# Feed-forward pairs by seven products: one bank for four of them, copies between on ScalarE, and other pairs

## The chip, the cores and the metric

The kernel runs on one core of a Trainium2 chip. The metric is device time in microseconds of one execution, on the device alone. The core's engines are TensorE (PE in the profile; its weight loads are PEld), VectorE (DVE), ScalarE (ACT), GpSimd (POOL) and SyncE (SP), which issues most transfers. Each engine works through its own queue in order, and semaphores hold an instruction until what it needs is there.

## The reference, cut to what matters

Two layers of a streaming encoder over 512 tokens of width 1024. Each has a mixer, a cross-attention to a memory and a gated feed-forward network with a short convolution along the tokens; the change touches the last one alone:

```python
def conv_ffn(xn, w_up, conv_w, conv_b, w_down):
    h = causal_depthwise_conv(xn @ w_up, conv_w) + conv_b
    g, u = jnp.split(h, 2, axis=-1)
    return (jax.nn.gelu(g) * u) @ w_down
...
        x = x + conv_ffn(rms_norm(x, ffn_norm[layer]), ffn_w_up[layer], ffn_conv_w[layer],
                         ffn_conv_b[layer], ffn_w_down[layer])
```

All is float32. w_up has 1024 rows and 2 x 2816 columns, so h has 44 blocks of 128 columns; block p of the gate half and block 22 + p of the other half are a pair, and there are 22 pairs. w_down takes the 22 blocks of the product back to 1024.

## The kernel before, in words

Everything is kept transposed: 128 features on the partitions, 512 tokens along the free axis. A float32 product is done as three matmuls (`mm3`, lines 285 to 291): each operand is split into a rounded high half (a cast on ScalarE) and the rest (a subtraction on VectorE, `sub`, line 279), and high x high, low x high and high x low are summed in a PSUM bank.

`ffn_steps` (line 1136) does a layer's feed-forward. It first lists tasks, each with an engine, an assumed duration, what it depends on, a priority (its due time) and buffer slots that it takes and frees; then `Sched.run` (line 181) simulates the engines and issues the instructions in the order that comes out. At each step it takes, over all engines, the task that can start first, by priority where several can. So the order of every engine's queue comes from the planner's durations, and TensorE's tasks of one pair can be put between those of another.

A pair is computed in one of two ways. `plain` (line 1308) runs two blocks of 8 x 3 matmuls of 512 tokens, each evacuated by one VectorE product with the norm's factor (line 1317). `seven` (line 1327) treats the pair as a 2 x 2 product (two column blocks by two halves of the 1024 rows, against two halves of the tokens) and does it with seven products of 4 x 3 matmuls of 256 tokens. It needs sums of weights: S2 and S4 (lines 1358 and 1364, VectorE) and f1, which GpSimd's queue adds up in a transfer (`onto`, line 1335, tile `sa`), and sums of the input, `th` and `tl`, which `forms` (line 1240) makes once per layer with two ScalarE scalings, three VectorE sums and a split per row block, four times.

In `seven` the products run in the order p1, p6, p2, a fill, p7, p5, a fill, p4, p3. Bank X takes p1 and p2, bank Y p6, p7 and p4, bank R p5 and p3. ScalarE copies p1 as v with its sign turned (line 1390) before p2 is added to it, and copies c11 out of X (line 1405). Every other partial result is a VectorE sum of a bank and a copy (`sum_`, line 1392): u2 and u3 go to buffers, c22, c21 and c12 to the rows of `hs`. p2 waits for v, p7 for u2, p4 for u3, p3 for c22, because each adds into a bank that must have been read before. Then one VectorE product scales all rows (line 1419), and `tail` does the convolution (ScalarE line 1274, four VectorE steps line 1281), the gelu (line 1289), the product (line 1291) and its split into `ah` and `al` (lines 1295 and 279).

A fill (line 1441) takes one block of the down projection from a queue: 4 x 3 matmuls of 512 with a 512-column cast, its low half and an add into x. The queue gets eight blocks at pairs 5, 9, 13 and 18; the last four are held back until after pair 21. Every pair from 5 on asks for two fills, so pairs 17, 20 and 21 find the queue empty. Pairs 4 to 15 and 17 to 20 go by `seven`, the others by `plain`. After the pairs come the four held blocks, then in layer one eight more blocks of six, and in layer two `finish` (line 1656), which needs the acts of pairs 16 to 21.

Of the kernel before, what the change touches and what calls it, by code (L numbers as in the profile page):

```python
# [13 lines left out]
ALU = mybir.AluOpType  # L14
# [8 lines left out]
NPAIR = DFF // P  # L23
CHUNKS = [(0, 4), (4, 4), (8, 4), (12, 4), (16, 6)]

SEVEN = (4, 5, 6, 7, 8, 9, 10, 11, 12, 13, 14, 15, 17, 18, 19, 20)
EPS = 1e-6

X_AT, X_STEP = 2.6, 0.6
# [37 lines left out]
def folded(ap):  # L67

    return ap.rearrange("p (r k) -> p r k", r=2)
# [168 lines left out]
class Builder:  # L238
# [897 lines left out]
    def ffn_steps(self, layer, mp):  # L1136
# [103 lines left out]
        def forms(k, at):  # L1240

            st = {}

            def scaled(j):
                if j == 0:
                    st["t"] = hs2[st["_hs"]][:, :, 2:514]
                nc.scalar.activation(st["t"][:, j, :512], self.x[k + 4 * j][:], AF.Identity, scale=self.col("ffn", layer * 8 + k + 4 * j))

            def first():
                st["r"] = raw_tile(st, "sa")[:]  # L1250
                tt_(out=pair(st["r"][:, :512]), in0=pair(st["t"][:, 0, :512]), in1=st["t"][:, :, 256:512], op=ALU.subtract)

            T1, T3, T2, T4 = (slice(256 * i, 256 * i + 256) for i in range(4))
            tt_ = nc.vector.tensor_tensor
            a = add("ACT", ACV, lambda: scaled(0), (), at, [("hs", st)])
            a = add("ACT", ACV, lambda: scaled(1), [a], at)
            a = add("DVE", tt(512), first, [a], at, [("sa", st)])
            a = add("DVE", tt(256), lambda: tt_(out=st["r"][:, T2], in0=st["t"][:, 1, 256:512], in1=st["r"][:, T1], op=ALU.add), [a], at)
            a = add("DVE", tt(256), lambda: tt_(out=st["r"][:, T4], in0=st["t"][:, 1, 0:256], in1=st["r"][:, T2], op=ALU.subtract), [a], at, (), [("hs", st)])
            h = add("ACT", act(1024), lambda: nc.scalar.copy(th[k][:], st["r"]), [a], at)  # L1260
            formed.append(add("DVE", tt(1024), lambda: self.sub(tl[k][:], st["r"], th[k][:]), [h], at, (), [("sa", st)]))

# [64 lines left out]
        def seven(p, fill):  # L1327
# [57 lines left out]
            n = 1.345  # L1385
            get = rows(st, at + 2.0)

            def v_():
                st["v_"] = self.til(mp, "v", (P, 256), bufs=1)
                nc.scalar.activation(folded(st["v_"][:]), bank("X")(), AF.Copy, scale=-1.0)  # L1390

            def sum_(tag, out, a, b, op):
                if tag:
                    st[tag] = self.til(mp, tag, (P, 256), bufs=1)
                tt_(out=out(), in0=a(), in1=b(), op=op)

            bank = lambda n_: (lambda: restored(st[n_][:, :256]))
            tmp = lambda n_: (lambda: folded(st[n_][:]))
            hs = lambda j, l: (lambda: folded(st["hs_"][:, j, 2 + 256 * l : 258 + 256 * l]))
            p1 = pe(n, lambda: opened("X", bx, "acc", f3, 0, *X(0, 0), "X", True), [w3], [("acc", bx)])  # L1400
            v = add("ACT", act(256), v_, [p1], clock[0], [("v", bv)])
            p6 = pe(n, lambda: opened("Y", by, "acc", s2, 0, *T2, "Y", True), [w2, *formed], [("acc", by)], [("s2", s2)])
            u2 = add("DVE", 0.33, lambda: sum_("u2", tmp("u2"), bank("Y"), tmp("v_"), ALU.add), [p6, v], clock[0], [("u2", bu2)])
            p2 = pe(n, lambda: product(f3, 512, *X(1, 0), "X", False), [p1, v], (), [("h", f3)])
            c11 = add("ACT", act(256), lambda: nc.scalar.copy(hs(0, 0)(), bank("X")()), [p2, get], clock[0] + 2.0, (), [("acc", bx)])
            fill()
            p7 = pe(n, lambda: product(f1, 0, *T3, "Y", False), [u2, w1])
            u3 = add("DVE", 0.33, lambda: sum_("u3", tmp("u3"), bank("Y"), tmp("v_"), ALU.add), [p7], clock[0], [("u3", bu3)])
            p5 = pe(n, lambda: opened("R", br, "s", f1, 512, *T1, "R", True), [w1], [("s", br)], [("h", f1)])
            c22 = add("DVE", 0.33, lambda: sum_(None, hs(1, 1), tmp("u3"), bank("R"), ALU.subtract), [u3, p5, get], clock[0], (), [("u3", bu3)])  # L1410
            fill()
            p4 = pe(n, lambda: product(a22, 0, *T4, "Y", False), [u3, w22], (), [("a22", a22)])
            c21 = add("DVE", 0.33, lambda: sum_(None, hs(1, 0), bank("Y"), tmp("v_"), ALU.add), [p4, get], clock[0] + 1.0, (), [("acc", by), ("v", bv)])
            p3 = pe(n, lambda: product(s4, 0, *X(1, 1), "R", False), [c22, w4], (), [("s4", s4)])
            c12 = add("DVE", 0.33, lambda: sum_(None, hs(0, 1), bank("R"), tmp("u2"), ALU.subtract), [p3, get], clock[0], (), [("s", br), ("u2", bu2)])

            def scaled():
                h = st["hs_"][:, :, 2:514]
# [29 lines left out]
        for p in range(22):  # L1448
            if p in due:
                queue += [(due[p], m) for m in range(8)]  # L1450
            if p == 19:
                queue, late = queue[:-4], queue[-4:]
            (seven if p in SEVEN else plain)(p, fill if p >= 5 else lambda: None)
            if p < 2:
                for k in (2 * p, 2 * p + 1):
                    forms(k, clock[0] + 4.0 * (k % 2))
# [376 lines left out]
```

## Time and profile before

| | |
|---|---|
| device time of the runs | 1451.02, 1455.0 and 1483.01 us, median 1455.0 |
| the profiled execution | 1451.45 us, its span 1449.6 us |
| granted TensorE clock, mean | 0.998 |
| TensorE, VectorE, ScalarE busy | 1423.5, 1189.9, 798.5 us |
| stretch 404.5 to 739.7 us (feed-forward of layer one) | 335.2 us: TensorE 329.73, VectorE 312.80, ScalarE 184.90 busy |
| stretch 1103.5 to 1406.7 us (pairs of layer two and the four held blocks) | 303.2 us: TensorE 298.80, VectorE 290.74, ScalarE 169.97 busy |

The profile is of one execution. Times within it count from the first instruction. A row of its timeline has the start, the duration, the engine, the line of the kernel, the operation, output and inputs by their names in the program with their shapes, and in brackets the idle time just before with what ended it. TensorE's matmuls are pipelined and their ends are modelled, so the next one can start before the end that is shown; the distance of two starts is the pace. VectorE's and ScalarE's instructions overlap their neighbours by a little too.

### The profile page before, as it was taken

How to read it: one execution, taken by the hardware profiler on the slowest of the kernel's cores; microseconds unless marked ns; L12 is line 12 of the kernel's file. 1: busy time of each engine (PE TensorE's matmuls, PEld its weight loads, DVE VectorE, ACT ScalarE, POOL GpSimd, SP SyncE). 2: the span in 40 equal slices, each digit the busy share in tenths (PEclk: the TensorE clock that was granted, in tenths of full speed). 3: DMA queues.
4: the chain of work that ended last, by engine and by line, in shares of the span. 5: the costliest groups of instructions: out<-in, count | busy, mean ns of one | idle time of the engine just before them, and what ended most of it. 6: DMA issues, size and time to landing. Idle time of an engine off the chain costs nothing.

```text
span 1449.6 us, 22210 instructions
## 1 busy us (share of the span) xinstructions
PE 1423.5 (98%) x8330; PEld 1266.7 (87%) x8330; DVE 1189.9 (82%) x2255; ACT 798.5 (55%) x1345; POOL 58.4 (4%) x100
## 2 busy tenths in 40 slices
PE   9999999999999999999999999999999999999998
PEld 7888868899888999989888788889988899998997
DVE  7778886766689999989778868677667999999985
ACT  7767574444466555545456734444445665554544
POOL 0000120000001000000000100000000000000000
PEclk9999999999999999999999999999999999999999
DMA  5222305323247565642332232324323765654322
GB/s 201 88 73 73 102 30 160 117 88 131 83 142 198 152 170 163 164 127 68 90 102 87 74 102 74 116 88 129 119 81 130 187 168 162 172 153 134 92 70 80
DMA packets 60795, 171.74 MB, mean 118 GB/s; under 512 B 6672, under 2 KB 6672, under 8 KB 60688
## 3 DMA queue, kind: packets, MB, share of 16 engines
q1 hardware_dynamic: 55072, 152.43, 32.5%
q0 software_dynamic: 4608, 16.78, 6.9%
q8 instruction: 65, 1.06, 0.3%
q10 hardware_dynamic: 1008, 1.12, 0.2%
q14 instruction: 42, 0.34, 0.1%
HBM read 168.21 MB, written 2.10 MB: 117 GB/s over the span
## 4 chain that ended last, share of the span: by engine, by line
PE 72%; DVE 19%; issue 4%; ACT 3%; DMA 2%; POOL 0%; SPq 0%; DVEq 0%; ACTq 0%; POOLq 0%
PE acc L289 14%; PE acc L291 14%; PE acc L290 14%; DVE wl L279 4%; PE w L289 4%; PE w L291 4%; PE w L290 4%; DVE c L1281 3%; PE acc L351 2%; PE acc L352 2%; PE acc L353 2%; PE s L289 2%; PE s L291 2%; PE s L290 2%; PE w L1620 1%
## 5 line engine op out<-in xcount | busy, mean ns | idle before, releaser
L289 PE MATMUL acc<-xh,wh 128*128 128x512 f32 (+1 forms) x832 | 293.6, 353 | 4.2 <-ACT v L1390 4.2
L291 PE MATMUL acc<-xh,wl 128*128 128x512 f32 (+1 forms) x832 | 289.0, 347 | 0.0
L290 PE MATMUL acc<-xl,wh 128*128 128x512 f32 (+1 forms) x832 | 289.0, 347 | 0.0
L279 DVE TENSOR_TENSOR wl<-raw,wh 128x1024 fp32r<-128x1024 f32 (+2 forms) x201 | 240.3, 1196 | 38.0 <-ACT wh L282 35.8
L282 ACT CAST wh<-raw 128x1024 fp32r<-128x1024 f32 (+2 forms) x137 | 140.3, 1026 | 155.8 <-PE acc L290 96.8
L289 PEld LDWEIGHTS acc<-xh,wh 128*128 128x128 f32 x832 | 158.2, 190 | 19.5 <-ACT v L1390 4.8
L291 PEld LDWEIGHTS acc<-xh,wl 128*128 128x128 f32 x832 | 158.1, 190 | 15.3
L290 PEld LDWEIGHTS acc<-xl,wh 128*128 128x128 f32 x832 | 158.3, 190 | 14.4
L1281 DVE SCALAR_TENSOR_TENSOR c<-hs,vec,c 128x512 f32<-128x512 f32 x176 | 128.8, 745 | 6.6 <-ACT c L1274 6.2
L289 PE MATMUL w<-ah,wh 128*128 128x512 f32 x304 | 115.4, 380 | 0.0
L290 PE MATMUL w<-al,wh 128*128 128x512 f32 x304 | 115.3, 379 | 0.0
L291 PE MATMUL w<-ah,wl 128*128 128x512 f32 x304 | 115.3, 379 | 0.0
L1274 ACT ACTIVATE c<-hs,vec 128x512 f32<-128x512 f32 x88 | 67.9, 808 | 64.2 <-DVE hs L1419 57.1
L291 PEld LDWEIGHTS w<-ah,wl 128*128 128x128 f32 x304 | 57.5, 189 | 8.1
L290 PEld LDWEIGHTS w<-al,wh 128*128 128x128 f32 x304 | 57.6, 190 | 6.7
L289 PEld LDWEIGHTS w<-ah,wh 128*128 128x128 f32 x304 | 57.7, 190 | 6.7
L1295 ACT CAST ah<-c 128x512 fp32r<-128x512 f32 x44 | 27.3, 620 | 65.7 <-DVE c L1291 65.6
L289 PE MATMUL acc<-mem,wh 128*128 128x256 f32 (+1 forms) x192 | 60.3, 314 | 0.0
L291 PE MATMUL acc<-mem,wl 128*128 128x256 f32 (+1 forms) x192 | 59.7, 311 | 0.0
L290 PE MATMUL acc<-mem,wh 128*128 128x256 f32 (+1 forms) x192 | 59.6, 311 | 0.0
L512 DVE TENSOR_TENSOR x<-w,x 128x512 f32<-128x512 f32 x72 | 49.1, 682 | 7.9 <-PE w L291 7.8
L512 DVE TENSOR_TENSOR x<-acc,x 128x512 f32<-128x512 f32 x32 | 22.0, 690 | 40.4 <-PE acc L291 40.4
(373 smaller groups left out, 3766.0 us busy)
## 6 DMA issues: line engine op xcount, KB each, us to landing
raw<-in_up_dram SPq DMA_DIRECT2D x56, 512.0 KB, 3.3
dr<-in_down_dram SPq DMA_DIRECT2D x64, 256.0 KB, 3.4
sa<-in_up_dram SPq DMA_DIRECT2D x32, 512.0 KB, 4.2
sa<-in_up_dram POOLq DMA_DIRECT2D x32, 512.0 KB, 5.5
raw<-in_xk_dram SPq DMA_DIRECT2D x16, 512.0 KB, 3.3
raw<-in_wo_dram SPq DMA_DIRECT2D x16, 512.0 KB, 3.3
raw<-in_xq_dram SPq DMA_DIRECT2D x16, 512.0 KB, 3.3
raw<-in_xv_dram SPq DMA_DIRECT2D x16, 512.0 KB, 3.3
```

Of the source, the lines that this page charges most:

```text
L279: self.nc.vector.tensor_tensor(out=lo, in0=v, in1=hi.bitcast(F32), op=ALU.subtract)
L282: self.nc.scalar.copy(hi, v)
L289: mm(out, wh, xh, start=first, stop=False, skip_group_check=parts)
L290: mm(out, wh, xl, start=False, stop=False, skip_group_check=parts)
L291: mm(out, wl, xh, start=False, stop=last, skip_group_check=parts)
L351: mm(ps, xh[k][:, ts], wh, start=(k == 0), stop=False)
L352: mm(ps, xh[k][:, ts], wl, start=False, stop=False)
L353: mm(ps, xl[k][:, ts], wh, start=False, stop=(k == 7))
L512: self.nc.vector.tensor_tensor(out=x, in0=restored(ps[:]), in1=x, op=ALU.add)
L1274: nc.scalar.activation(st["c_"][:, j, :], hs()[:, j, 2:514], AF.Identity, scale=self.col("cw", (layer * 3 + 2) * 44 + blk), bias=self.col( ...
L1281: nc.vector.scalar_tensor_tensor(out=c, in0=hs()[:, j, n : n + 512], scalar=w, in1=c, op0=ALU.mult, op1=ALU.add)
L1295: nc.scalar.copy(acts[p][0][:], u())
```

## The change

Bank Y now takes p1, p6, p7 and p4 one after the other. The signs in `forms` are chosen so that the bank itself holds each partial result; ScalarE copies it out between the products: v (p1), u2, u3 with the sign turned, and c21 with the sign turned straight into `hs`. Bank X holds p2 alone and VectorE adds v to it for c11; c22 and c12 stay VectorE sums. The order becomes p1, p2, p6, a fill, p5, p7, a fill, p4, p3; p6 waits for v, p7 for u2, p4 for u3, p3 for c22. In `forms` one VectorE difference of 512 columns becomes two of 256, and the two sums become operations with a factor of -1. The pairs by `seven` become 5 to 20 in layer one and 5 to 21 in layer two; so pair 4 is plain, pair 16 is by seven, and pair 21 too in layer two. The planner gets the new durations, dependencies and slots, and makes its order anew.

```diff
--- before.py
+++ after.py
@@ -23,7 +23,7 @@
 NPAIR = DFF // P
 CHUNKS = [(0, 4), (4, 4), (8, 4), (12, 4), (16, 6)]
 
-SEVEN = (4, 5, 6, 7, 8, 9, 10, 11, 12, 13, 14, 15, 17, 18, 19, 20)
+SEVEN = (range(5, 21), range(5, 22))
 EPS = 1e-6
 
 X_AT, X_STEP = 2.6, 0.6
@@ -1248,15 +1248,19 @@
 
             def first():
                 st["r"] = raw_tile(st, "sa")[:]
-                tt_(out=pair(st["r"][:, :512]), in0=pair(st["t"][:, 0, :512]), in1=st["t"][:, :, 256:512], op=ALU.subtract)
+                tt_(out=st["r"][:, T1], in0=st["t"][:, 0, 0:256], in1=st["t"][:, 0, 256:512], op=ALU.subtract)
+                tt_(out=st["r"][:, T3], in0=st["t"][:, 1, 256:512], in1=st["t"][:, 0, 256:512], op=ALU.subtract)
+
+            def second(to, a, b):
+                nc.vector.scalar_tensor_tensor(out=st["r"][:, to], in0=st["r"][:, a], scalar=-1.0, in1=st["t"][:, 1, b], op0=ALU.mult, op1=ALU.subtract)
 
             T1, T3, T2, T4 = (slice(256 * i, 256 * i + 256) for i in range(4))
             tt_ = nc.vector.tensor_tensor
             a = add("ACT", ACV, lambda: scaled(0), (), at, [("hs", st)])
             a = add("ACT", ACV, lambda: scaled(1), [a], at)
-            a = add("DVE", tt(512), first, [a], at, [("sa", st)])
-            a = add("DVE", tt(256), lambda: tt_(out=st["r"][:, T2], in0=st["t"][:, 1, 256:512], in1=st["r"][:, T1], op=ALU.add), [a], at)
-            a = add("DVE", tt(256), lambda: tt_(out=st["r"][:, T4], in0=st["t"][:, 1, 0:256], in1=st["r"][:, T2], op=ALU.subtract), [a], at, (), [("hs", st)])
+            a = add("DVE", 2 * tt(256), first, [a], at, [("sa", st)])
+            a = add("DVE", 0.4, lambda: second(T2, T1, slice(256, 512)), [a], at)
+            a = add("DVE", 0.4, lambda: second(T4, T2, slice(0, 256)), [a], at, (), [("hs", st)])
             h = add("ACT", act(1024), lambda: nc.scalar.copy(th[k][:], st["r"]), [a], at)
             formed.append(add("DVE", tt(1024), lambda: self.sub(tl[k][:], st["r"], th[k][:]), [h], at, (), [("sa", st)]))
 
@@ -1385,34 +1389,33 @@
             n = 1.345
             get = rows(st, at + 2.0)
 
-            def v_():
-                st["v_"] = self.til(mp, "v", (P, 256), bufs=1)
-                nc.scalar.activation(folded(st["v_"][:]), bank("X")(), AF.Copy, scale=-1.0)
-
-            def sum_(tag, out, a, b, op):
-                if tag:
-                    st[tag] = self.til(mp, tag, (P, 256), bufs=1)
+            def copied(tag, scale):
+                st[tag] = self.til(mp, tag, (P, 256), bufs=1)
+                nc.scalar.activation(folded(st[tag][:]), bank("Y")(), AF.Copy, scale=scale)
+
+            def sum_(out, a, b, op):
                 tt_(out=out(), in0=a(), in1=b(), op=op)
 
             bank = lambda n_: (lambda: restored(st[n_][:, :256]))
             tmp = lambda n_: (lambda: folded(st[n_][:]))
             hs = lambda j, l: (lambda: folded(st["hs_"][:, j, 2 + 256 * l : 258 + 256 * l]))
-            p1 = pe(n, lambda: opened("X", bx, "acc", f3, 0, *X(0, 0), "X", True), [w3], [("acc", bx)])
-            v = add("ACT", act(256), v_, [p1], clock[0], [("v", bv)])
-            p6 = pe(n, lambda: opened("Y", by, "acc", s2, 0, *T2, "Y", True), [w2, *formed], [("acc", by)], [("s2", s2)])
-            u2 = add("DVE", 0.33, lambda: sum_("u2", tmp("u2"), bank("Y"), tmp("v_"), ALU.add), [p6, v], clock[0], [("u2", bu2)])
-            p2 = pe(n, lambda: product(f3, 512, *X(1, 0), "X", False), [p1, v], (), [("h", f3)])
-            c11 = add("ACT", act(256), lambda: nc.scalar.copy(hs(0, 0)(), bank("X")()), [p2, get], clock[0] + 2.0, (), [("acc", bx)])
+            AC = 0.42
+            p1 = pe(n, lambda: opened("Y", by, "acc", f3, 0, *X(0, 0), "Y", True), [w3], [("acc", by)])
+            v = add("ACT", AC, lambda: copied("v", 1.0), [p1], clock[0], [("v", bv)])
+            p2 = pe(n, lambda: opened("X", bx, "acc", f3, 512, *X(1, 0), "X", True), [w3], [("acc", bx)], [("h", f3)])
+            c11 = add("DVE", 0.33, lambda: sum_(hs(0, 0), bank("X"), tmp("v"), ALU.add), [p2, v, get], clock[0] + 2.0, (), [("acc", bx), ("v", bv)])
+            p6 = pe(n, lambda: product(s2, 0, *T2, "Y", False), [w2, v, *formed], (), [("s2", s2)])
+            u2 = add("ACT", AC, lambda: copied("u2", 1.0), [p6], clock[0], [("u2", bu2)])
             fill()
-            p7 = pe(n, lambda: product(f1, 0, *T3, "Y", False), [u2, w1])
-            u3 = add("DVE", 0.33, lambda: sum_("u3", tmp("u3"), bank("Y"), tmp("v_"), ALU.add), [p7], clock[0], [("u3", bu3)])
-            p5 = pe(n, lambda: opened("R", br, "s", f1, 512, *T1, "R", True), [w1], [("s", br)], [("h", f1)])
-            c22 = add("DVE", 0.33, lambda: sum_(None, hs(1, 1), tmp("u3"), bank("R"), ALU.subtract), [u3, p5, get], clock[0], (), [("u3", bu3)])
+            p5 = pe(n, lambda: opened("R", br, "s", f1, 512, *T1, "R", True), [w1], [("s", br)])
+            p7 = pe(n, lambda: product(f1, 0, *T3, "Y", False), [u2, w1], (), [("h", f1)])
+            u3 = add("ACT", AC, lambda: copied("u3", -1.0), [p7], clock[0], [("u3", bu3)])
+            c22 = add("DVE", 0.33, lambda: sum_(hs(1, 1), tmp("u3"), bank("R"), ALU.subtract), [u3, p5, get], clock[0], (), [("u3", bu3)])
             fill()
             p4 = pe(n, lambda: product(a22, 0, *T4, "Y", False), [u3, w22], (), [("a22", a22)])
-            c21 = add("DVE", 0.33, lambda: sum_(None, hs(1, 0), bank("Y"), tmp("v_"), ALU.add), [p4, get], clock[0] + 1.0, (), [("acc", by), ("v", bv)])
+            c21 = add("ACT", AC, lambda: nc.scalar.activation(hs(1, 0)(), bank("Y")(), AF.Copy, scale=-1.0), [p4, get], clock[0] + 1.0, (), [("acc", by)])
             p3 = pe(n, lambda: product(s4, 0, *X(1, 1), "R", False), [c22, w4], (), [("s4", s4)])
-            c12 = add("DVE", 0.33, lambda: sum_(None, hs(0, 1), bank("R"), tmp("u2"), ALU.subtract), [p3, get], clock[0], (), [("s", br), ("u2", bu2)])
+            c12 = add("DVE", 0.33, lambda: sum_(hs(0, 1), bank("R"), tmp("u2"), ALU.add), [p3, get], clock[0], (), [("s", br), ("u2", bu2)])
 
             def scaled():
                 h = st["hs_"][:, :, 2:514]
@@ -1450,7 +1453,7 @@
                 queue += [(due[p], m) for m in range(8)]
             if p == 19:
                 queue, late = queue[:-4], queue[-4:]
-            (seven if p in SEVEN else plain)(p, fill if p >= 5 else lambda: None)
+            (seven if p in SEVEN[layer] else plain)(p, fill if p >= 5 else lambda: None)
             if p < 2:
                 for k in (2 * p, 2 * p + 1):
                     forms(k, clock[0] + 4.0 * (k % 2))
```

## The prediction

> **What bounds the kernel now.** I read the page first (span, busy shares, slices), then the stretches of the two feed-forward stages, then TensorE's rows one by one with what released each late one.
>
> ```profile
> span 1449.6 us, 22210 instructions
> ...
> PE 1423.5 (98%) x8330; PEld 1266.7 (87%) x8330; DVE 1189.9 (82%) x2255; ACT 798.5 (55%) x1345; POOL 58.4 (4%) x100
> ...
> DVE  7778886766689999989778868677667999999985
> ACT  7767574444466555545456734444445665554544
> ```
>
> TensorE is busy for 98% of the span. VectorE stands at 9 in the slices of the two feed-forward stages (404 to 740 us and 1103 to 1407 us) and at 6 to 8 elsewhere. A window over one period of a middle pair, one pair's seven products with two blocks of the down projection, and one over each disturbed end, show how close the two engines run there. The columns are busy time and count by engine, then clock, DMA share and GB/s.
>
> ```profile
> core 0: us, PE busy (x) PEld busy (x) DVE busy (x) ACT busy (x) POOL busy (x), PEclk, DMA share, GB/s
> 447.00:462.00 15.00, 12.16 (x101) 11.59 (x100) 13.76 (x22) 7.69 (x14) 1.70 (x2) 1.00 0.80 197
> 547.59:562.17 14.58, 14.58 (x111) 13.85 (x109) 14.51 (x24) 8.11 (x14) 0.84 (x1) 1.00 0.62 160
> 1337.00:1351.00 14.00, 11.78 (x103) 11.39 (x102) 12.32 (x20) 6.94 (x13) 0.87 (x1) 1.00 0.56 150
> ```
>
> In the middle TensorE is never idle (14.58 of 14.58 us) and VectorE hardly is (14.51); ScalarE has 6.5 us free. At the two ends TensorE loses time. TensorE's pace is read from the starts of its products:
>
> ```profile
> 567.53 0.38 PE L289 MATMUL w<-ah,wh 128*128 128x512 f32 x1
> ...
> 570.12 0.27 PE L289 MATMUL acc<-th,wh 128*128 128x256 f32 x1
> ...
> 571.46 0.28 PE L289 MATMUL s<-th,wh 128*128 128x256 f32 x1
> ```
>
> Twelve matmuls of 512 columns take 570.12 - 567.53 = 2.59 us, twelve of 256 columns 571.46 - 570.12 = 1.34 us. A seven-product pair (84 of 256) is then 7 x 1.34 = 9.38 us, a plain pair (48 of 512) 4 x 2.59 = 10.36 us. All late products of the pairs, with the idle time and its releaser in brackets:
>
> ```profile
> 449.89 0.28 PE L291 MATMUL s<-th,wl 128*128 128x256 f32 x1
> 452.86 0.38 PE L289 MATMUL acc<-xh,wh 128*128 128x256 f32 x1 [2.69 <-ACT v L1390]
> ...
> 531.56 0.38 PE L289 MATMUL acc<-th,a22h 128*128 128x256 f32 x1 [0.40 <-DVE u L1395]
> ...
> 620.90 0.38 PE L289 MATMUL s<-xh,s4h 128*128 128x256 f32 x1 [0.29 <-DVE hs L1395]
> ...
> 643.82 0.38 PE L289 MATMUL acc<-th,wh 128*128 128x256 f32 x1 [1.71 <-DVE u L1395]
> ...
> 1150.22 0.38 PE L289 MATMUL acc<-xh,wh 128*128 128x256 f32 x1 [1.05 <-ACT v L1390]
> ...
> 1228.94 0.38 PE L289 MATMUL acc<-th,a22h 128*128 128x256 f32 x1 [0.42 <-DVE u L1395]
> ...
> 1318.32 0.38 PE L289 MATMUL s<-xh,s4h 128*128 128x256 f32 x1 [0.33 <-DVE hs L1395]
> ...
> 1338.65 0.38 PE L289 MATMUL acc<-xh,wh 128*128 128x256 f32 x1 [0.51 <-ACT v L1390]
> ...
> 1341.98 0.38 PE L289 MATMUL acc<-th,wh 128*128 128x256 f32 x1 [1.72 <-DVE u L1395]
> ```
>
> The brackets sum to 9.12 us. A bracket counts from a row's modelled end (0.28 us) though the next matmul could start after 0.11, so each of the nine hides 0.17 us more: 10.7 us in all. The first layer's 452.86 and the second's 1150.22 belong to the start of the seven-product pairs (pair 4, which has no fill); 531.56 and 1228.94 are single late u3; 620.90, 643.82, 1318.32, 1338.65 and 1341.98 lie around plain pair 16 and pair 17, which has no fill either. So the stage is at TensorE's pace, with 10.7 us of stalls that VectorE, or ScalarE behind it, causes.
>
> **The change part by part.** *TensorE's work.* Pair 4 becomes plain and pair 16 seven in both layers: they cancel. Pair 21 of layer two becomes seven: 9.38 - 10.36 = **-0.98 us**. Its loads grow from 1024 to 1792 KB on SP's and POOL's queues, and pair 16's likewise; the middle window above carries just that load (0.62 of the DMA engines) with no stall of TensorE, so I price the transfers at nothing. If that cover were gone, up to a whole load's landing would show, the last column here (us):
>
> ```profile
> raw<-in_up_dram SPq DMA_DIRECT2D x56, 512.0 KB, 3.3
> ...
> sa<-in_up_dram POOLq DMA_DIRECT2D x32, 512.0 KB, 5.5
> ```
>
> *Sums moved between engines.* Per pair VectorE loses u2, u3 and c21 and gets c11, five sums to three; ScalarE goes from two copies to four.
>
> ```profile
> L1395 DVE TENSOR_TENSOR u<-acc,v x64: 409/417/424, 457.3 to 1385.3; 128x256 f32<-128x256 f32 x64
> ```
>
> ```profile
> L1390 ACT ACTIVATE v<-acc x32: 360/383/392, 452.4 to 1378.1; 128x256 f32<-128x256 f32 x32
> ...
>   PE acc L291: 15.8, 19
>   DVE hs L1395: 6.4, 6
> ```
>
> ```profile
> 1376.87 0.41 DVE L1395 TENSOR_TENSOR hs<-acc,v 128x256 f32<-128x256 f32 x1
> 1377.20 0.68 DVE L279 TENSOR_TENSOR a22l<-ra,a22h 128x512 fp32r<-128x512 f32 x1
> 1377.80 0.41 DVE L1395 TENSOR_TENSOR hs<-s,u 128x256 f32<-128x256 f32 x1
> ```
>
> A queued sum takes its engine for 0.33 us (1377.20 - 1376.87), a 512 one for 0.60; two sums less are 0.66 us a pair. VectorE's load with fills falls from 14.51 to 13.85 us against TensorE's 14.58; ScalarE's rises from 8.11 by at most 2 x 0.38 to 8.87 and stays clear.
> [...]
>
> *The new chain of waits in the one bank.* p6 waits for v, p7 for u2, p4 for u3. How long one such link takes is seen where p2 waits for v today:
>
> ```profile
> 564.74 0.28 PE L291 MATMUL acc<-xh,wl 128*128 128x256 f32 x1
> ...
> 565.05 0.38 ACT L1390 ACTIVATE v<-acc 128x256 f32<-128x256 f32 x1 [0.83 <-PE acc L291]
> ...
> 566.19 0.28 PE L289 MATMUL acc<-xh,wh 128*128 128x256 f32 x1
> ```
>
> The product's last matmul leaves at 564.85, the copy ends at 565.43, the next user starts at 566.19: a link of 0.58 us under 1.34 us of cover, 0.76 spare. After the change v has p2 as cover (1.34), u2 has a fill and p5 (3.93, before only a fill), u3 a fill (2.59, before p5 and a fill), c22 a fill and p4. With fills all of that is covered: 0. In pairs without a fill (17 and 20, and 21 of layer two) u3's link stands bare before p4: 0.58 us each, unless the planner slips the next pair's first product between. Five of them are 0 to 2.9 us; I take 0.5, since the planner issues any product that can start. Queued behind a waiting copy on ScalarE are weight casts and the tail's activations, with 5.7 us to spare a period.
>
> *Start of the seven-product pairs.* Now pair 5, which has fills of 2.59 us in it. VectorE has one plain pair's time more to finish the forms, whose two new instructions of 256 cost at most what a 512 one does (0.60 us) and at least 0.33; eight forms' extra lies under plain pairs: 0. The two start stalls (2.69 + 1.05 + 0.34 = 4.1 us) go down to 1.0: **-3.1**. Bounds 0 and -4.1. Next late would be the load that pair 5's sum waits for, seen today in this row:
>
> ```profile
> 450.39 0.69 DVE L1358 TENSOR_TENSOR sb<-sa,raw 128x512 f32<-128x512 f32 x1 [1.24 <-DMA sa<-in_up_dram]
> ```
>
> *Late u3 in the middle* (0.40 + 0.42 + 0.34 = 1.2 us): u3 leaves VectorE's full queue. Bounds 0 and -1.2; **-0.8**.
>
> *Pairs 15 to 17* (0.29 + 1.71 + 0.33 + 0.51 + 1.72 + 5 x 0.17 = 5.4 us): the switch from seven to plain and back goes, pair 17 without fills stays. There VectorE needs 14.51 - 4 x 0.60 (two down casts' lows and two adds into x of 512) = 12.1 us, 11.4 after, against 9.38. Bounds +1 and -5.4; **-2.7**.
>
> *Pairs 20 and 21 of layer two, and the end.* Both have no fill. VectorE's need is 2 x 11.4 = 22.8 against 18.8 us of TensorE: 4.0 us too much, which the four late blocks (4 x 2.59 = 10.4 us against 4 x 1.2 of VectorE) give back afterwards. Before, pair 21 was plain: two lows of 1024 columns, two evacuations and six steps of the tail of 512, together twelve slots of 512 at 0.60, 7.2 us; so VectorE gets 22.8 - 12.1 - 7.2 = 3.5 us more.
>
> ```profile
> 1404.68 0.68 DVE L279 TENSOR_TENSOR al<-c,ah 128x512 fp32r<-128x512 f32 x1
> ```
>
> ```profile
> 1406.71 0.38 PE L289 MATMUL acc<-ah,wh 128*128 128x512 f32 x1
> ```
>
> Pair 21's last act half is there at 1405.36; the finish starts at 1406.71 and uses it after 15 more matmuls (3.2 us): 4.6 us spare, which the 3.5 us more of VectorE and the 0.98 us earlier TensorE nearly use up. Bounds 0 and +5.6 (4.0 and 1.6 at the finish); **+1.5** by the window of pair 17 above, where VectorE's deficit showed as about 2 us.
>
> **Sum.** -0.98 - 3.1 - 0.8 - 2.7 + 0.5 + 1.5 = -5.6 us. The profiled execution took 1451.45 us (span 1449.6 and 1.85 around it): 1451.45 - 5.6 = **1446 us**. It stands 3.5 us under the median of the runs shown, 1455.0, and beside their lowest, 1451.02; I forecast such an undisturbed time.
>
> **The rivals.** *The stalls stay* because loads cause them (the 1.24 us above): only 0.98 us is won, 1450.5. Against it: most brackets name VectorE or ScalarE. *All go:* -0.98 - 10.7 gives 1440; for it the middle pairs without a stall, against it the pairs without fills. *Layer two's end decides:* if pairs 20 and 21 and the finish cost their whole 5.6 us and half of the other gains (3.3) fails to come, the time is 1451.45 - 0.98 - 3.3 + 5.6 + 0.5 = 1453. *ScalarE's queue, the one that ends slower by over 2%:* ScalarE works in order, and its activation of the tail waits for VectorE's scaled rows:
>
> ```profile
> ACT c L1274 <- DVE hs L1419: 57.1, 28, 4.5
> ```
>
> That is 2.0 us a time. A copy of the Y chain queued behind it costs nothing up to 0.76 us of lateness, then all of it: (2.0 - 0.76) x 33 = 41 us, 1492. It passes 2% (29 us) from 1.64 us of lateness in every pair. Against it: v stands in the same queue now, and its rows show 15.8 us of idle time for TensorE's product itself against 6.4 for VectorE.
>
> **How the numbers follow.** Forecast 0.55 (its own range 1442 to 1450), stalls stay 0.17, all go 0.13, layer two's end 0.10, ScalarE's queue 0.05. The range 1439 to 1457 takes in all but the last, with the bounds: lowest -12, highest +5.6. A measurement of this kernel tells about 2% (29 us) from no change. No case reaches 1426, since work and stalls together are 12 us: faster 0.01. Slower 0.05 is ScalarE's queue; within 2% 0.94.
>
> **What would show it.** Right: VectorE's window in a middle pair near 13.9 us with TensorE still full; no stall over 1 us at pair 5; pairs 16 and 17 with under 3 us of stalls per layer; a stall of 0.5 to 2 us at pairs 20 and 21 of layer two; twelve matmuls still 1.34 and 2.59 us. Wrong: p6, p7 or p4 late behind a ScalarE copy in the middle pairs; a start stall that only moved from pair 4 to pair 5 behind a load; a late first product of the finish.

## The result, and the profile after

| | before | after |
|---|---|---|
| median of the runs side by side, us | 1450.91 | 1456.57 (1455.0 to 1458.3) |
| profiled execution, us | 1451.45 | 1456.26 |
| its span, us | 1449.6 | 1454.5 |
| granted TensorE clock, mean | 0.998 | 0.993 |

The ratio after to before is 1.0040, 95% interval 1.0027 to 1.0052: the change made the kernel slower by 4 to 8 us, where 5.6 us less were forecast. The time lies within the range given, its sign is the opposite one.

The page of after, the rows of the engines:

```profile
span 1454.5 us, 22322 instructions
...
PE 1423.8 (98%) x8366; PEld 1269.8 (87%) x8366; DVE 1177.4 (81%) x2206; ACT 826.3 (57%) x1416; POOL 58.7 (4%) x101
```

VectorE is 12.5 us less busy and ScalarE 27.8 us more, as intended, and TensorE's busy time stands still although the span grew by 4.9 us. By these rows the growth is idle time. (Matmuls that run slower count as busy: from 470 to 480 us TensorE is busy for 10.00 of 10.00 us at a clock of 0.91; they are found below.) The windows of after show where it isn't and where it is; the columns after the name of the stretch are its length, the busy time of TensorE, weight loads, VectorE, ScalarE and GpSimd, the granted clock, the DMA share and the rate:

```profile
569.17:583.73 14.56, 14.56 (x110) 13.92 (x109) 14.03 (x22) 9.01 (x15) 0.85 (x1) 1.00 0.63 170
...
620.00:650.00 30.00, 30.00 (x237) 29.04 (x236) 29.33 (x44) 19.10 (x32) 1.71 (x2) 1.00 0.56 150
450.00:460.00 10.00, 10.00 (x55) 8.95 (x54) 6.83 (x11) 4.31 (x6) 0.00 (x0) 1.00 0.51 119
460.00:470.00 10.00, 3.19 (x21) 3.00 (x20) 9.13 (x16) 5.25 (x10) 0.86 (x1) 0.75 0.42 127
470.00:480.00 10.00, 10.00 (x61) 9.23 (x61) 7.98 (x13) 4.91 (x8) 0.00 (x0) 0.91 0.54 137
1160.00:1170.00 10.00, 3.71 (x27) 3.52 (x27) 9.13 (x14) 5.58 (x9) 0.86 (x1) 0.73 0.36 111
```

The same 30 us in the kernel before, around its pairs 15 to 17:

```profile
620.00:650.00 30.00, 28.00 (x181) 25.69 (x180) 26.39 (x40) 13.77 (x22) 0.87 (x1) 1.00 0.44 131
```

A middle pair (first row) is as forecast: TensorE full, VectorE at 14.03 of 14.56 us. Pairs 15 to 17 (second row) have no stall left, where before had 2.0 us. All the loss is at the start of the pairs by seven: TensorE works 3.19 of the 10 us from 460 to 470, and the clock granted there is 0.75. In layer two it is the same again at 1160.

TensorE's timeline of after at that place (bracket: idle time before the instruction, and what ended it):

```profile
460.97 0.28 PE L291 MATMUL acc<-xh,wl 128*128 128x256 f32 x1
468.05 0.58 PE L289 MATMUL acc<-th,s2h 128*128 128x256 f32 x1 [6.81 <-ACT v L1394]
468.42 0.42 PE L290 MATMUL acc<-tl,s2h 128*128 128x256 f32 x1
468.64 0.42 PE L291 MATMUL acc<-th,s2l 128*128 128x256 f32 x1
...
470.77 0.63 PE L289 MATMUL w<-ah,wh 128*128 128x512 f32 x1
471.20 0.63 PE L290 MATMUL w<-al,wh 128*128 128x512 f32 x1
471.62 0.46 PE L291 MATMUL w<-ah,wl 128*128 128x512 f32 x1
471.92 0.38 PE L289 MATMUL w<-ah,wh 128*128 128x512 f32 x1
```

Pair 5's p6 starts 6.97 us after TensorE was ready (6.46 in layer two), and then the matmuls run at half pace: 256 columns every 0.21 us instead of 0.11, 512 every 0.43 instead of 0.22, until 471.9. Twelve of 256 and three of 512 take 3.87 us instead of 1.99: another 1.9 us. In layer two the half pace lasts some 2.9 us behind a stall of 6.46 and costs another 1.5 us.

The bracket names the copy v, but that is only the last in a row. VectorE's waits between 404 and 520 us, after and then before (total, times, longest):

```profile
DVE sb L1362 <- DMA sa<-in_up_dram: 6.9, 2, 4.5
```

```profile
DVE sb L1358 <- DMA sa<-in_up_dram: 1.5, 2, 1.2
```

VectorE's queue stands at the weight sums of pairs 5 and 6 until their transfers `sa` land:

```profile
450.81 0.69 DVE L1362 TENSOR_TENSOR sb<-sa,raw 128x512 f32<-128x512 f32 x1 [4.50 <-DMA sa<-in_up_dram]
...
454.46 0.69 DVE L1362 TENSOR_TENSOR sb<-sa,raw 128x512 f32<-128x512 f32 x1 [2.35 <-DMA sa<-in_up_dram]
```

Behind them in VectorE's queue are the plain pairs' evacuations and tails; ScalarE's convolutions wait for those, and v stands behind the convolutions in ScalarE's queue:

```profile
465.69 0.81 ACT L1278 ACTIVATE c<-hs,vec 128x512 f32<-128x512 f32 x1 [0.76 <-DVE al L279]
466.41 0.60 ACT L1183 CAST wh<-dr 128x512 fp32r<-128x512 f32 x1
466.92 0.81 ACT L1278 ACTIVATE c<-hs,vec 128x512 f32<-128x512 f32 x1
467.64 0.36 ACT L1394 ACTIVATE v<-acc 128x256 f32<-128x256 f32 x1
```

Why `sa` is late is seen in SP's queue, after and then before (start, stretch, number of issues):

```profile
413.67 23.20 SPq L1169 DMA_DIRECT2D raw<-in_up_dram  x5
436.96 1.69 SPq L1169 DMA_DIRECT2D sa<-in_up_dram  x2
```

```profile
413.82 16.50 SPq L1169 DMA_DIRECT2D raw<-in_up_dram  x4
431.16 5.42 SPq L1169 DMA_DIRECT2D sa<-in_up_dram  x2
```

Before, four raw loads of the plain pairs go out and then the first `sa` load. After, a fifth raw load stands ahead of it, waits until 436.54 for its buffer (the split `wl` at line 279, which reads that buffer, ends on VectorE at 436.51), and holds the `sa` load back by 5.8 us. GpSimd's accumulating transfers follow, after and then before:

```profile
442.91 1.00 POOL L1340 DMA_DIRECT2D sa<-in_up_dram  x1 [70.58 <-PE acc L290]
444.22 0.86 POOL L1340 DMA_DIRECT2D sa<-in_up_dram  x1 [0.31 <-DVE c L1285]
```

```profile
436.53 1.00 POOL L1336 DMA_DIRECT2D sa<-in_up_dram  x1 [64.29 <-DVE tl L279]
442.29 0.86 POOL L1336 DMA_DIRECT2D sa<-in_up_dram  x1 [4.75 <-DVE c L1281]
```

The first starts 6.4 us later, the second 1.9, and so the two fall together. In SP's rows above an issue that waits holds up the one behind it: the `sa` load goes at 436.96 us, 0.42 us after the raw load that waited until 436.54, and without that raw load ahead of it, in the kernel before, at 431.16. That the `sa` load could have gone 8 us earlier is shown below, by the run that moves it to another queue.

### The profile page after: what moved, and what is told of

Its sections match the earlier page's. It is cut to its first block, busy times and chain, and to the rows that moved or that the text cites. A ratio compares the mean times of both kernels' runs of the same rounds, so it can differ in the third digit from the quotient of the medians.

```text
span 1454.5 us, 22322 instructions
## 1 busy us (share of the span) xinstructions
PE 1423.8 (98%) x8366; PEld 1269.8 (87%) x8366; DVE 1177.4 (81%) x2206; ACT 826.3 (57%) x1416; POOL 58.7 (4%) x101
## 4 chain that ended last, share of the span: by engine, by line
PE 78%; DVE 13%; ACT 4%; issue 3%; DMA 2%; POOL 0%; SPq 0%; DVEq 0%; ACTq 0%; POOLq 0%
PE acc L289 15%; PE acc L291 14%; PE acc L290 14%; PE w L289 5%; PE w L290 5%; PE w L291 5%; DVE wl L279 3%; PE s L289 2%; PE s L290 2%; PE s L291 2%; PE acc L351 2%; PE acc L352 2%; PE acc L353 2%; DVE c L1285 2%; DMA sa<-in_up_dram 1%
## 5 line engine op out<-in xcount | busy, mean ns | idle before, releaser
L289 PE MATMUL acc<-xh,wh 128*128 128x512 f32 (+1 forms) x824 | 289.2, 351 | 0.0
L291 PE MATMUL acc<-xh,wl 128*128 128x512 f32 (+1 forms) x824 | 285.0, 346 | 0.0
L290 PE MATMUL acc<-xl,wh 128*128 128x512 f32 (+1 forms) x824 | 284.8, 346 | 0.0
```

What stands on the lines that cost most here:

```text
L289: mm(out, wh, xh, start=first, stop=False, skip_group_check=parts)
L290: mm(out, wh, xl, start=False, stop=False, skip_group_check=parts)
L291: mm(out, wl, xh, start=False, stop=last, skip_group_check=parts)
```

## The experiments

Three theories. **L**: the loads for the first pairs by seven are late, and VectorE's queue stands at sb for them. **S**: the new chain of sums and copies, or pair 5 itself, makes the start late. **F**, formed after the first four runs: the new sign operations in `forms` turn the order in SP's queue, and all else follows. Each run was compared with the kernel before on the same chip; its median there was 1450.39 in the first four, 1449.43 in the next four, 1449.39 in the last four. "Start stall" is the idle time of TensorE in the first pairs by seven, as the distance of two matmuls beyond their pace.

### Old sums, new pairs

The kernel before with the new sets of pairs:

```diff
-SEVEN = (4, 5, 6, 7, 8, 9, 10, 11, 12, 13, 14, 15, 17, 18, 19, 20)
+SEVEN = (range(5, 21), range(5, 22))
```

> The old sums and signs, the new set of pairs (5 to 20, 5 to 21). Theory L, the loads: VectorE's queue stands at the weight sums sb of pairs 5 and 6 until the accumulating transfers into sa have landed, whatever the sums are; the start stall at pair 5 is again 5 to 8 us in each layer, VectorE waits 5 to 7 us per layer for sa, and the time is 1455 to 1460 us (the middle pairs lose VectorE's relief besides). Rival S, the new chain of sums: v, copied by ScalarE behind the tail's activations, is what p6 waits for, so with the old order the start stall is under 3 us per layer and the time 1449 to 1452 us.

Measured: 1447.69 us (1444.99 to 1454.06), ratio 0.9983 (0.9966 to 1.0001). The time lies under the ranges of both theories; the profile is of the fastest of its ten executions. Start stalls 2.00 and 1.42 us, waits at sb 1.3 us, SP's queue with four raw loads ahead of the first `sa` (429.95). So the later first pair doesn't make the start late. L as first put, with loads late whatever the sums are, is refuted.

### New sums, old pairs

The changed kernel with the old set of pairs in both layers:

```diff
-SEVEN = (range(5, 21), range(5, 22))
+SEVEN = ((4, 5, 6, 7, 8, 9, 10, 11, 12, 13, 14, 15, 17, 18, 19, 20),) * 2
```

> The new sums and signs, the old set of pairs (4 to 15, 17 to 20). Theory L: the start stalls are as in the kernel before (2.9 and 1.2 us, up to 1 us either way), the late u3 of the middle and part of the stalls at pairs 15 to 17 go, and the time is 1446 to 1450 us against 1450.9 before. Rival S: the start stall is 5 to 8 us in each layer at pair 4 too, with TensorE's pace halved behind it, and the time is 1455 to 1460 us.

Measured: 1452.09 us (1450.84 to 1453.83), ratio 1.0009 (0.9999 to 1.0018). Start stalls 0.92 + 2.16 and 1.01 + 2.15 us with a granted clock of 0.83 in 450 to 470, waits at sb of 4.2 and 4.5 us, and five raw loads ahead of the first `sa` (435.69). The time lies between the ranges of the two theories. The late load came with the code of the sums, not with the pairs.

### New sums from pair 4 on

```diff
-SEVEN = (range(5, 21), range(5, 22))
+SEVEN = (range(4, 21), range(4, 22))
```

> The changed kernel with pair 4 by seven products as well: pairs 4 to 20, in layer two 4 to 21. TensorE's work falls by 2 x 0.98 us more. Theory L: the start stalls are those of the kernel before (2.9 and 1.2 us, up to 1 us either way), no clock loss follows them, the middle stays free of stalls, and the time is 1450.9 - 2.9 of work - 5 to 7 of stalls, 1441 to 1444 us. Rival S: the start stall stays at 5 to 8 us per layer, the time is 1453 to 1456 us.

Measured: 1448.16 us (1446.69 to 1450.8), ratio 0.9985 (0.9975 to 0.9994). Start stalls 1.58 + 1.02 + 2.16 + 0.83 and 0.69 + 2.15 + 0.84 us, granted clock 1.00, waits at sb 6.0 and 4.0 us, five raw loads first (`sa` at 435.33). Neither theory had this time. The late load is there, but beside the changed kernel the start stalls sum to 9.3 us instead of 13.4, no halved pace follows them, and one pair more in each layer is done by seven (2 x 0.98 us).

### One buffer for the weight sums

```diff
-        RAWS = {"raw": (self.wp, 1024, 3), "dr": (mp, 512, 2), "sa": (mp, 1024, 3), "sb": (mp, 512, 2), "ra": (mp, 512, 2)}
+        RAWS = {"raw": (self.wp, 1024, 3), "dr": (mp, 512, 2), "sa": (mp, 1024, 3), "sb": (mp, 512, 1), "ra": (mp, 512, 2)}
```

and the planner's `sb=2` became 1.

> The changed kernel with one buffer for sb instead of two, so that pair 6's weight sum can't stand in VectorE's queue before pair 5's halves s2 and s4 are made. Theory L: VectorE's second wait for sa (2.4 and 2.5 us) goes, the first (4.5 and 3.8 us) stays; the start stalls fall from 7.0 and 6.5 to 4 to 5 us each, and the time by 4 to 6 us to 1450 to 1453 us, less if the middle pairs miss the second buffer. Rival S: the start stalls stay at 6.5 to 7 us and the time at 1456 to 1458 us.

Measured: 1452.36 us (1451.15 to 1456.35), ratio 1.0016 (1.0005 to 1.0027). Start stalls 4.14 and 4.68 us, waits at sb 3.5 and 4.1 us and one instead of two of them per layer. With one buffer the next pair's sum can't stand in VectorE's queue ahead of the plain pair's work, and 4 us come back, as L says of this part of the chain. The `sa` load stays late (436.00).

### Old forms in the changed kernel

```diff
-                tt_(out=st["r"][:, T1], in0=st["t"][:, 0, 0:256], in1=st["t"][:, 0, 256:512], op=ALU.subtract)
-                tt_(out=st["r"][:, T3], in0=st["t"][:, 1, 256:512], in1=st["t"][:, 0, 256:512], op=ALU.subtract)
+                tt_(out=pair(st["r"][:, :512]), in0=pair(st["t"][:, 0, :512]), in1=st["t"][:, :, 256:512], op=ALU.subtract)
```

and the two operations with a factor as the plain sums of before, with the planner's durations of before.

> The changed kernel with the three VectorE sums of the input forms as they were before (one difference of 512 columns, two plain sums); the signs of three of the four input sums are then not those that the new products need, so the values of the seven-product pairs differ from the reference, while every duration, wait and load stays. Theory F (the new forms' instructions bring a weight load of a plain pair ahead of the two first sa loads in SP's queue, and all that follows is late by it): the sa loads are issued near 430 us again, VectorE waits under 2 us at the weight sums sb, the start stall falls from 7 us to 1 to 3 us in each layer with no slow pace behind it, and the time is 1444 to 1448 us. Rival S (the start is late because of the new chain of sums and copies, or because pair 5 asks more of VectorE than pair 4 did): the start stall stays at 5 to 7 us, 1454 to 1458 us.

Measured: 1445.55 us (1441.65 to 1451.56), ratio 0.9969 (0.9954 to 0.9984). Start stalls 2.17 and 2.03 us. SP's queue of this kernel:

```profile
412.58 16.49 SPq L1169 DMA_DIRECT2D raw<-in_up_dram  x4
429.91 5.41 SPq L1169 DMA_DIRECT2D sa<-in_up_dram  x2
```

The old order is back, and 10 us with it (1.0040 - 0.9969 = 0.71% of 1450). S is refuted. One thing was not as expected: the pace behind the stall was halved here too, shown in the last section.

### New forms alone

The kernel before with the new `forms` and nothing else of the change (the same lines the other way round).

> The kernel before with only the new input forms (two differences of 256 columns and two sums with a factor of -1); old chain of sums, old pairs. Three of the four input sums change sign, so the values of the seven-product pairs differ from the reference. Theory F: the sa loads stand behind a fifth raw load in SP's queue and go out near 436 us instead of 431, VectorE's waits at sb grow from 1.5 to 3 us or more, the first seven-product pair stalls for 4 us or more per layer, and the time is 1452 to 1456 us. Rival S (forms of the same length cost nothing; the start belongs to the sums): sb waits stay under 2 us, start stalls as before, 1450 to 1451 us.

Measured: 1459.81 us (1457.95 to 1462.48), ratio 1.0065 (1.0041 to 1.0089). SP's queue:

```profile
412.15 23.20 SPq L1169 DMA_DIRECT2D raw<-in_up_dram  x5
435.44 14.75 SPq L1169 DMA_DIRECT2D sa<-in_up_dram  x4
```

Start stalls 0.65 + 1.01 + 2.49 and 0.68 + 1.01 + 2.48 us, clock 0.91 and 0.83 in the 20 us around them. The new operations in a layer's four forms, with nothing else of the change, cost 6 to 13 us, more than F expected.

### One load on GpSimd's queue

The changed kernel, complete; pair 5's first `sa` load leaves SP's queue:

```diff
-            b1 = load(sa, "sa", up2[p][:, :, :512], 1024, at - 20.0)
+            b1 = load(sa, "sa", up2[p][:, :, :512], 1024, at - 20.0, "POOL" if p == 5 else "SP")
```

(`load` issues it with `nc.gpsimd.dma_start`, and the planner counts it on that engine.)

> The changed kernel, complete, with one thing moved: the first sa load of pair 5 is issued by GpSimd's queue instead of SP's, so that it cannot stand behind SP's raw loads. Theory F: VectorE's wait for pair 5's sum falls from 4.5 to under 2 us, the start stall from 7 to 3 us or less in each layer, the pace stays whole, and the time is 1446 to 1450 us. Rival S: VectorE meets the next late thing at once, the stall keeps 5 us or more, 1454 to 1457 us. Third case: GpSimd's queue, which works in order too, holds the load behind its own earlier instruction, the load lands no earlier than before, and nothing changes (1456).

Measured: 1439.17 us (1437.94 to 1440.84), ratio 0.9921 (0.9895 to 0.9947), 7 us below the range that F expected. GpSimd's queue, and the windows around the start in both layers:

```profile
428.93 0.88 POOL L1171 DMA_DIRECT2D sa<-in_up_dram  x1 [56.61 <-DVE sa L1257]
432.99 0.88 POOL L1342 DMA_DIRECT2D sa<-in_up_dram  x1 [3.19 <-DMA sa<-in_up_dram]
```

```profile
450.00:470.00 20.00, 20.00 (x123) 18.36 (x122) 18.77 (x27) 11.09 (x18) 0.85 (x1) 1.00 0.52 137
1150.00:1170.00 20.00, 20.00 (x152) 19.19 (x151) 17.89 (x28) 12.61 (x23) 1.72 (x2) 1.00 0.63 168
```

The load goes as soon as the forms free its buffer, 8.0 us earlier than after (436.96), and its accumulation 9.9 us earlier. No wait at sb is left, no start stall, and no lowered clock. SP's queue still has its five raw loads in a row (413.65, 23.20 us): it is not their order that costs, but what stands behind them.

### From pair 4 on, with the loads on GpSimd's queue

The pairs 4 to 20 (4 to 21 in layer two), and `"POOL" if p in (4, 5)`.

> The changed kernel, complete, with seven products from pair 4 on in both layers (4 to 20, and 4 to 21 in layer two), and the first sa loads of pairs 4 and 5 issued by GpSimd's queue. The version from pair 4 without the moved loads ran at 1448.2 us, with start stalls of 5.6 and 3.7 us in the two layers and waits of 6.0 and 4.0 us at sb. Theory F: those waits fall under 2 us each, the start stalls to 1 to 3 us, and the time is 1442 to 1446 us, below every kernel so far. Rival S: the start stalls stay and the time is 1447 to 1450 us.

Measured: 1438.10 us (1438.01 to 1439.11), ratio 0.9915 (0.9895 to 0.9936), 4 us below the range that F expected. No stall at pairs 4 and 5, one of 0.7 us in each layer at 483.28 and 1175.40; VectorE is busy without a break from 450 to 470 us (20.00 of 20.00 us). It is not clearly apart from the run above: a pair more by seven saves TensorE 0.98 us a layer, and VectorE's full queue takes most of that back.

### Which part of the forms turns the order

Two theories: F1, the order turns by the one VectorE instruction more in each form, and F2, by the operations with a factor. Three kernels part them. First, plain second sums, with the two differences of 256 kept:

```diff
-                nc.vector.scalar_tensor_tensor(out=st["r"][:, to], in0=st["r"][:, a], scalar=-1.0, in1=st["t"][:, 1, b], op0=ALU.mult, op1=ALU.subtract)
+                tt_(out=st["r"][:, to], in0=st["r"][:, a], in1=st["t"][:, 1, b], op=ALU.subtract)
```

> The changed kernel with the two operations with a factor of -1 in the forms made plain differences again; the two differences of 256 columns stay two instructions. Two of the four input sums then have other signs, so the values of the seven-product pairs differ from the reference. If it is the one instruction more per form that turns the order in SP's queue (theory F1), this is like the changed kernel: five raw loads ahead of the sa loads, start stalls of 6 to 7 us, 1454 to 1458 us. If it is the operation with a factor (theory F2), the sa loads go out near 430 us, the start stall is 2 to 3 us and the time 1443 to 1448 us.

One difference of 512, with the factors kept (the diff of the old forms above, its first part alone):

> The changed kernel with the two differences of 256 columns made one of 512 again; the two operations with a factor of -1 stay. One of the four input sums then has the other sign, so the values of the seven-product pairs differ from the reference. Theory F1 (the one instruction more per form): the sa loads go out near 430 us ahead of the fifth raw load, the start stall falls to 2 to 3 us per layer, 1443 to 1448 us. Theory F2 (the operation with a factor): as the changed kernel, 1454 to 1458 us.

And a complete kernel with other signs, so that one difference makes both T1 and T3:

```diff
+                tt_(out=pair(st["r"][:, :512]), in0=st["t"][:, :, 256:512], in1=pair(st["t"][:, 0, :512]), op=ALU.subtract)
...
-            c22 = add("DVE", 0.33, lambda: sum_(hs(1, 1), tmp("u3"), bank("R"), ALU.subtract), [u3, p5, get], clock[0], (), [("u3", bu3)])
+            c22 = add("DVE", 0.33, lambda: sum_(hs(1, 1), tmp("u3"), bank("R"), ALU.add), [u3, p5, get], clock[0], (), [("u3", bu3)])
...
-            c12 = add("DVE", 0.33, lambda: sum_(hs(0, 1), bank("R"), tmp("u2"), ALU.add), [p3, get], clock[0], (), [("s", br), ("u2", bu2)])
+            c12 = add("DVE", 0.33, lambda: sum_(hs(0, 1), tmp("u2"), bank("R"), ALU.subtract), [p3, get], clock[0], (), [("s", br), ("u2", bu2)])
```

(S4 with its sign turned, by an operation with the factor -1; T2 with the factor 1, T4 with -1.)

> The changed kernel, complete, with other signs: T1 and T3 both turned so that one VectorE difference of 512 columns makes both, the sum S4 of the weights turned as well, and c22 and c12 taken with the other sign. As many instructions as the kernel before has in the forms, all loads on SP's queue. Theory F1: as the kernel with the old forms, sa loads ahead of the fifth raw load, start stalls of 2 to 3 us, 1443 to 1448 us. Theory F2 or S: 1454 to 1458 us.

Measured: plain second sums 1456.98 us (1455.47 to 1458.96), ratio 1.0054 (1.0036 to 1.0072), start stalls 7.09 and 6.41. One difference 1449.09 (1443.06 to 1452.39), ratio 0.9994 (0.9982 to 1.0006), stalls 3.18 and 3.04. Other signs 1447.68 (1444.67 to 1451.87), ratio 0.9990 (0.9977 to 1.0003), stalls 2.40 and 2.75. SP's queue in the first and in the third of them:

```profile
413.37 23.20 SPq L1169 DMA_DIRECT2D raw<-in_up_dram  x5
436.66 1.24 SPq L1169 DMA_DIRECT2D sa<-in_up_dram  x2
```

```profile
412.69 16.50 SPq L1169 DMA_DIRECT2D raw<-in_up_dram  x4
430.03 5.42 SPq L1169 DMA_DIRECT2D sa<-in_up_dram  x2
```

It is the one instruction more per form, not the factor (F1). With the order of before back, the complete change (other signs) is not clearly faster than the kernel before: its start stalls are still 2.4 and 2.8 us, with a clock of 0.83 from 460 to 470. The kernel with one difference came out 1.1 us above the range expected of it, with a stall of 3 us as expected and executions 9 us apart. Over all twelve runs, and in both layers, every kernel with two differences has five raw loads ahead of its SP queue's first `sa`, and every one with one difference has four.

### Pair 21 of layer two

The kernel with the load on GpSimd's queue, with `SEVEN = (range(5, 21), range(5, 21))`.

> The changed kernel with pair 5's first sa load on GpSimd's queue (it ran at 1439.2 us), and pair 21 of layer two plain again, all else the same. It prices pair 21 by seven where nothing else is late. By the prediction's steps pair 21 by seven saves 0.98 us of TensorE work and costs up to 1 us where it and pair 20 stand without fills, so plain should be within 1 us of 1439.2: 1438.5 to 1440.2. Rival (VectorE's load of pairs 20 and 21 by seven holds the finish or its blocks): plain is faster by 1.5 us or more, 1435 to 1437.7.

Measured: 1437.91 us (1437.62 to 1438.3), ratio 0.9920 (0.9904 to 0.9936), and 1.3 us under the same with pair 21 by seven, which ran beside other runs of before (1449.43 against 1449.39). From pair 18's p3 to the first matmul of the finish, with pair 21 plain and then by seven:

```profile
1346.93 0.38 PE L289 MATMUL s<-xh,s4h 128*128 128x256 f32 x1 [0.19 <-DVE hs L1399]
...
1393.03 0.38 PE L289 MATMUL acc<-ah,wh 128*128 128x512 f32 x1
```

```profile
1348.46 0.38 PE L289 MATMUL s<-xh,s4h 128*128 128x256 f32 x1 [0.22 <-DVE hs L1399]
...
1370.35 0.38 PE L289 MATMUL acc<-th,wh 128*128 128x256 f32 x1 [0.36 <-ACT u L1396]
...
1380.35 0.38 PE L289 MATMUL acc<-th,wh 128*128 128x256 f32 x1 [0.36 <-ACT u L1396]
...
1394.83 0.38 PE L289 MATMUL acc<-ah,wh 128*128 128x512 f32 x1
```

46.10 us against 46.37: by seven the pair wins 0.98 us of work and loses it again, since p7 waits 0.53 us for the copy u2 in each of the two pairs without fills. The rest of the 1.3 us lies ahead of pair 18 in the two profiles (1348.46 against 1346.93), 1.50 of it already at the start of layer one's feed-forward, where the kernels don't differ. So the pair costs some 0.3 us, and the time of it alone isn't settled by the medians.

## Why the prediction was wrong, point by point

**The step that failed** is "Start of the seven-product pairs", -3.1, bounds 0 to -4.1, and in it the sentence that eight forms' extra "lies under plain pairs: 0". As VectorE time this was right. But the extra instruction turned the order of SP's queue, which the step didn't look at: the start stalls rose from 4.7 to 13.4 us in both layers together, and time lost in small pieces rose by 2.8 us, where the halved pace alone adds 1.9 + 1.5. That is +11.5 us in place of -3.1. The prediction had named the load that "next late would be", at the right instruction (sb behind sa), and had listed a stall moved to pair 5 behind a load among the things that would make it wrong; but it took the load's time of before for fixed, and its rival of loads ended at "only 0.98 us is won". No bound of the step went above zero. That the time still lies in the range is luck: the range's upper end, 1457, was made of the 5.6 us of layer two's end, which cost 1.0.

The other terms, as after and the runs showed them:

| step | forecast | measured in the profiles |
|---|---|---|
| TensorE's work, pair 21 | -0.98 | not apart from its waits: together +0.3 |
| start | -3.1 | +8.7 stall, +2.8 in small pieces |
| late u3 in the middle | -0.8 | -1.1, both stalls gone (531.56 and 1228.94 before), with the old sums too |
| pairs 15 to 17 | -2.7 | -4.6: 5.4 gone, 0.4 a layer new at pair 18's p3 (665.03) |
| bare u3 links | +0.5 | 0, no row waits for u3 |
| pairs 20, 21 and the finish | +1.5 | +1.0, p7 behind u2 twice, and no stall in the finish |

With the -0.98 and two stalls of 0.3 us that went ahead of the pairs, the right column sums to +5.2 against the spans' +4.9. Without the start the terms gave -2.5 and the profiles show -5.7 (-0.98 - 1.1 - 4.6 + 1.0): the sizes were right in direction but for the bare u3 links, which cost nothing, and the gain of pairs 15 to 17 was sized too small. Two of the runs part what brought it. New pairs with old sums stall for 1.45 us a layer behind pair 17 (before, 2.3 and 3.1 around it), new sums with old pairs for 1.66 us, and both together for 0.4: each half does some. The late u3 of the middle is gone in both of these runs, with the old sums too, so that part isn't shown to come from moving u3 to ScalarE. The kernel with the load on GpSimd's queue adds up the same way: 4.7 us of start stalls gone and these 5.7 make 10.4, and it ran 10.3 us under before (1439.17 against 1449.43).

One working doesn't come out: the 1.6 us at the finish, in the bound of layer two's end, follow from none of the figures beside them; no stall was seen there.

The rivals: *the stalls stay because of loads* was nearest in mechanism, but the loads came later than before, not as before. *All go*, 1440 us, is about what the complete change does once its load has left SP's queue (1439.2); with the load on SP's queue in the old order (other signs) it is 1447.7. *Layer two's end decides* cost 1.0 of its 5.6 us. *ScalarE's queue* is there at the start alone: with the loads in the old order p6 still waited 2.01 us for v in layer one, with v queued behind two convolutions; in the middle pairs no p6, p7 or p4 is late.

How the one instruction turns the order is shown in part. The kernel with one difference leaves every task, duration, dependency and slot of the planner as in the changed kernel, only the code that one task emits is different, and yet the order is the old one. So it isn't the planner's durations; it is made behind the planner, where the framework turns what was issued into SP's queue. By what rule the framework does so isn't shown.

## What to carry to other kernels

Read an in-order load queue at each place where an edit moves a buffer's release or adds an instruction to its user, even when the engine's time is hidden: here a raw load that waited for its buffer until 436.54 us held the `sa` load behind it until 436.96, and one short instruction more in each of four forms a layer cost some 7 to 10 us (1456.57 against the kernels with other signs and with the old forms). A first user with a long chain (load, accumulate, sum, split) should not share a queue with loads that wait for buffers of other work; moved from SP's queue to GpSimd's, one such load a layer was worth 17 us (1456.57 against 1439.17). And follow a bracket's releaser back through the in-order queues to the first wait before calling it the cause: here TensorE named ScalarE, ScalarE stood behind VectorE, and VectorE behind a transfer.

## What the runs showed of the hardware

In these profiles a stall cost more than its length where TensorE's pace dropped behind it. After 6.97 us of idle time in the kernel after it was half for 3.9 us and cost another 1.9, after 6.46 us it was half for some 2.9 and cost another 1.5; after 4.14 us with one sb buffer the clock of the 20 us from 450 was 0.91. But it dropped behind 2.17 us of idle time in one kernel too, and behind 2.9 us in another it did not. The first is the kernel with the old forms:

```profile
461.95 0.38 PE L289 MATMUL acc<-th,s2h 128*128 128x256 f32 x1 [2.01 <-ACT v L1390]
462.17 0.28 PE L290 MATMUL acc<-tl,s2h 128*128 128x256 f32 x1
462.28 0.34 PE L291 MATMUL acc<-th,s2l 128*128 128x256 f32 x1
462.41 0.42 PE L289 MATMUL acc<-th,s2h 128*128 128x256 f32 x1
```

From the fourth matmul on the pace is half: the next two start at 462.63 and 462.84, 0.21 to 0.22 us apart. The window 460 to 470 shows a clock of 0.83, by which some 3.4 us of the ten went at half pace, an estimate (10 x 0.17 / 0.5). The second is the kernel before: pair 4's stall (2.69 in its bracket) left the clock of 450 to 470 at 1.00, and so did 1.58 + 1.02 + 2.16 + 0.83 us in the kernel from pair 4 on. So in these profiles neither one stall's length nor their sum decides, and no run shows what does. Executions of one kernel differ too, and with the clock: the ten with old sums and new pairs go from 1444.99 us at a clock of 0.999 to 1454.06 at 0.994. So one profile doesn't say what a stall costs on the whole; the median over many executions does.
